# Interleaved RoPE on one core: row 2 stored and row 5 loaded in sixteen alternating pieces

## The chip, the cores and the metric

The kernel runs on one core of a Trainium2 chip. The metric is the device time of one execution in microseconds; before the change the median of three runs is 316.26 us (316.24 to 316.33). In the profile DVE is VectorE, ACT is ScalarE, POOL is GpSimd, SP is SyncE. POOL and SP issue the transfers of this kernel, each on a queue of its own (q0 is POOL's, q1 is SP's); sixteen DMA engines carry them out.

## The reference

The kernel rotates pairs of neighbouring elements (rotary position embedding, interleaved form). The input `x` has 8 batch rows of 2048 positions, 16 heads and 64 elements, in fp32; one batch row is 8 MB.

```python
x1 = x_pairs[..., 0]; x2 = x_pairs[..., 1]      # neighbours along the head dimension
out1 = x1 * cos - x2 * sin                      # cos, sin: [2048, 32], the same for all batches and heads
out2 = x1 * sin + x2 * cos
out = np.stack([out1, out2], axis=-1).reshape(batch, seq_len, num_heads, head_dim)
```

## The kernel before

A batch row is spread over 128 partitions, each of which holds K = 16 neighbouring positions: 16 x 1024 elements, a contiguous 64 KB in DRAM and 32 KB in SBUF, where the data lie in bf16. Transfers on POOL's queue convert between fp32 and bf16 on the way. SBUF has five slots for batch rows (`xt`); row b lives in slot `HOME[b]`, with `HOME = [0, 1, 2, 3, 4, 0, 1, 2]`. So rows 5, 6 and 7 take the slots of rows 0, 1 and 2 once those have been stored. In what follows rows count from 0: the third row is row 2, the sixth is row 5.

`load(b, n)` (L63) and `store(b, n)` (L67) each issue a single DMA on POOL for n whole rows. `rotate` does a row with three VectorE instructions: a product with the sine table into a work tile (L82), a product in place with the cosine table (L83), and their sum, with neighbours swapped (L88).

The order is written out by hand; each engine runs its instructions in the order of the program, and waits for what an instruction needs:

- SP loads the first four positions of row 0 in fp32 (L92). POOL issues the rest of row 0 (L93), cos and sin (L94, L95), rows 1 and 2 as one transfer, row 3, then row 4 in two parts (L98, L99).
- VectorE builds the tables (L103 to L105) and rotates row 0. A one-element copy on ScalarE (L111, L112) holds back `store(0, 1)` until the loads are nearly over; a one-element copy on POOL (L116, `mark`) waits for the last part of row 4.
- After it POOL issues `store(1, 2)`, `load(5, 1)`, `load(6, 2)`. `load(5, 1)` needs slot 0, so it waits for the store of row 0; `load(6, 2)` needs slots 1 and 2, so it waits for the store of rows 1 and 2.
- Rows 3 and 4 are rotated and stored as one transfer, rows 5 and 6 likewise, and row 7 in two parts: 12 positions from POOL (L127), and the last four through an fp32 tile and SP (L132, L133). L131 holds that last copy back until rows 5 and 6 are stored.

Of the kernel before, what the change touches and what calls it, by code (L numbers as in the profile page):

```python
# [2 lines left out]

# [4 lines left out]


@with_exitstack  # L10
def kernel(
    ctx: ExitStack,
    tc: tile.TileContext,
    x: bass.AP,
    cos: bass.AP,
    sin: bass.AP,
    out: bass.AP,
):
    nc = tc.nc
    fp32 = mybir.dt.float32  # L20
    bf16 = mybir.dt.bfloat16
    mult = mybir.AluOpType.mult
    add = mybir.AluOpType.add

    B, S, H, D = x.shape
    P = 128
    K = S // P
    KP = 16
    D2 = D // 2
    HD = H * D  # L30
    NX = 5
    HEAD = 4
    TAIL = 4
    LAST = 2


    HOME = [0, 1, 2, 3, 4, 0, 1, 2]

    x_t = x.rearrange("b (p k) h d -> b p k (h d)", p=P, k=K)
    out_t = out.rearrange("b (p k) h d -> b p k (h d)", p=P, k=K)  # L40
    x_r = x.rearrange("b (p k) h d -> p b (k h d)", p=P, k=K)
    out_r = out.rearrange("b (p k) h d -> p b (k h d)", p=P, k=K)
    cos_t = cos.rearrange("(p k) c -> p (k c)", p=P, k=K)
    sin_t = sin.rearrange("(p k) c -> p (k c)", p=P, k=K)

    consts = ctx.enter_context(tc.tile_pool(name="consts", bufs=1))
    stage = ctx.enter_context(tc.tile_pool(name="stage", bufs=1))

    xt = consts.tile([P, NX, K * HD], bf16)
    cos_sb = consts.tile([P, K * D2], fp32)  # L50
    sin_sb = consts.tile([P, K * D2], fp32)
    c_tab = consts.tile([P, K, D], bf16)
    s_tab = consts.tile([P, K, D], bf16)

    gate = consts.tile([1, 1], bf16)
    mark = consts.tile([1, 1], bf16)

    def home(b, k0=0, k1=K):
        return xt[:, HOME[b], k0 * HD : k1 * HD].rearrange("p (k c) -> p k c", c=HD)

    def load(b, n):
        h = HOME[b]
        nc.gpsimd.dma_start(out=xt[:, h : h + n], in_=x_r[:, b : b + n])  # L63

    def store(b, n):
        h = HOME[b]
        nc.gpsimd.dma_start(out=out_r[:, b : b + n], in_=xt[:, h : h + n])  # L67

    def rotate(b, k0=0, k1=K):
        nk = k1 - k0  # L70
        xp = home(b, k0, k1)
        qt = stage.tile([P, KP, HD], bf16, name="qt", tag="work")

        def rows(a):
            return a.rearrange("p k (h e) -> p k h e", h=H, e=D)

        def tab(a):
            return dataclasses.replace(
                a, offset=a.offset + k0 * D, ap=[a.ap[0], [D, nk], [0, H], [1, D]]
            )  # L80

        nc.vector.tensor_tensor(out=rows(qt[:, :nk]), in0=rows(xp), in1=tab(s_tab), op=mult)  # L82
        nc.vector.tensor_tensor(out=rows(xp), in0=rows(xp), in1=tab(c_tab), op=mult)  # L83
        q_swap = dataclasses.replace(
            qt, offset=qt.offset + 1, ap=[qt.ap[0], [2, nk * HD // 2], [-1, 2]]
        )
        x3 = xp.rearrange("p k (a j) -> p (k a) j", j=2)
        nc.vector.tensor_tensor(out=x3, in0=x3, in1=q_swap, op=add)  # L88

    with tc.manual_schedule():  # L90
        head = stage.tile([P, TAIL, HD], fp32, name="st", tag="work")
        nc.sync.dma_start(out=head[:, :HEAD], in_=x_t[0, :, :HEAD])  # L92
        nc.gpsimd.dma_start(out=home(0, HEAD), in_=x_t[0, :, HEAD:])  # L93
        nc.gpsimd.dma_start(out=cos_sb, in_=cos_t)  # L94
        nc.gpsimd.dma_start(out=sin_sb, in_=sin_t)  # L95
        load(1, 2)
        load(3, 1)
        nc.gpsimd.dma_start(out=home(4, 0, K - LAST), in_=x_t[4, :, : K - LAST])  # L98
        nc.gpsimd.dma_start(out=home(4, K - LAST), in_=x_t[4, :, K - LAST :])  # L99

        nc.scalar.copy(out=home(0, 0, HEAD), in_=head[:, :HEAD])  # L101
        s2 = s_tab.rearrange("p k (i j) -> p (k i) j", j=2)
        nc.vector.tensor_copy(out=s2[:, :, 0], in_=sin_sb)  # L103
        nc.vector.tensor_scalar_mul(s2[:, :, 1], sin_sb, -1.0)  # L104
        nc.vector.tensor_copy(  # L105
            out=c_tab.rearrange("p k (i j) -> p (k i) j", j=2),
            in_=cos_sb.to_broadcast([P, K * D2, 2]),
        )
        rotate(0, 0, HEAD)
        rotate(0, HEAD, K)  # L110
        nc.scalar.copy(out=gate, in_=home(4, K - LAST - 1, K - LAST)[:1, 0, :1])  # L111
        nc.scalar.copy(out=xt[:1, HOME[0], :1], in_=xt[:1, HOME[0], :1])  # L112
        store(0, 1)
        rotate(1)
        rotate(2)
        nc.gpsimd.tensor_copy(out=mark, in_=xt[:1, 4, K * HD - 1 :])  # L116
        store(1, 2)
        load(5, 1)
        load(6, 2)
        rotate(3)  # L120
        rotate(4)
        store(3, 2)
        for b in range(5, B):
            rotate(b)
            if b == 6:
                store(5, 2)
        nc.gpsimd.dma_start(out=out_t[B - 1, :, : K - TAIL], in_=home(B - 1, 0, K - TAIL))  # L127

        tail = stage.tile([P, TAIL, HD], fp32, name="st", tag="work")
        last = home(B - 1, K - TAIL, K)  # L130
        nc.scalar.copy(out=xt[:1, HOME[B - 2], :1], in_=xt[:1, HOME[B - 1], K * HD - 1 :])  # L131
        nc.scalar.copy(out=tail, in_=last)  # L132
        nc.sync.dma_start(out=out_t[B - 1, :, K - TAIL :], in_=tail)  # L133


# [1 line left out]
_INS = ['x', 'cos', 'sin']  # L137
_OUTS = [((8, 2048, 16, 64), 'float32')]


# [23 lines left out]
```

## Time and profile before

| | |
|---|---|
| median of three runs | 316.26 us (316.24 to 316.33) |
| span of the profiled execution, first to last instruction | 314.4 us |
| around it (median less span) | 1.8 us |
| VectorE busy | 210.4 us, 67% |
| ScalarE busy | 8.9 us, 3% |
| POOL busy | 13.9 us, 4%, 19 instructions |
| DMA | 102.24 MB written in 2816 packets, mean 325 GB/s |
| HBM | 67.63 MB read, 67.11 MB written, 429 GB/s |

The profile gives no time of its own for the profiled execution beside its span; the 1.8 us are what the median of the timed runs has on top. The GB/s of the DMA rows count the bytes that are written: 4 MB for a row that is loaded to bf16, 8 MB for one that is stored in fp32. On POOL and SP an instruction DMA_DIRECT2D is the issue of a transfer, not the transfer.

### The profile page before, as it was taken

What the parts mean: (1) busy time and instruction counts of PE and PEld (TensorE: products, weight loads), DVE (VectorE), ACT (ScalarE), POOL (GpSimd) and SP (SyncE); (2) the same over time, 40 slices, a digit from 0 to 9 for tenths busy, and PEclk for the clock granted to TensorE, in tenths of its full rate; (3) what the DMA queues carried; (4) which work ended last, traced back from release to release, by engine and by line L of the source; (5) the groups of instructions that cost most, each with busy time, mean ns of one, the idle gap of its engine ahead of it and who ended that gap; (6) DMA issues with size and microseconds to landing.
All of it is one profiled execution on the core that took longest, in us unless ns stands there. A gap on an engine that the chain in (4) does not pass through costs nothing.

```text
span 314.4 us, 116 instructions
## 1 busy us (share of the span) xinstructions
DVE 210.4 (67%) x30; ACT 8.9 (3%) x6; POOL 13.9 (4%) x19
## 2 busy tenths in 40 slices
DVE  0009995099999999999992399903999999200000
ACT  1040000000000000000000000000000000000400
POOL 5000000000002400000000000000000000000000
DMA  7999999999999999999999999999999999999997
GB/s 254 263 283 200 200 200 267 200 200 213 229 233 258 425 509 400 400 459 475 400 200 246 221 200 200 254 213 333 400 525 409 400 400 525 409 400 400 434 434 333
DMA packets 2816, 102.24 MB, mean 325 GB/s; under 512 B 256, under 2 KB 256, under 8 KB 512
## 3 DMA queue, kind: packets, MB, share of 16 engines
q0 software_dynamic: 2528, 98.04, 96.8%
q1 hardware_dynamic: 288, 4.19, 3.3%
HBM read 67.63 MB, written 67.11 MB: 429 GB/s over the span
## 4 chain that ended last, share of the span: by engine, by line
another core or an unknown queue 87%; DMA 5%; ACT 1%; ACTq 1%; issue 0%
DMA st<-in_x_dram 5%; ACT xt L101 1%; ACTq L159 1%; ACT xt L131 0%; ACT xt L112 0%; ACTq L131 0%; ACT gate L111 0%
## 5 line engine op out<-in xcount | busy, mean ns | idle before, releaser
L82 DVE TENSOR_TENSOR qt<-xt,s_tab 128x16384 bf16<-128x16384 bf16 (+2 forms) x9 | 69.7, 7743 | 34.4 <-DMA xt<-in_x_dram 34.3
L83 DVE TENSOR_TENSOR xt<-xt,c_tab 128x16384 bf16<-128x16384 bf16 (+2 forms) x9 | 69.7, 7744 | 0.4
L88 DVE TENSOR_TENSOR xt<-xt,qt 128x16384 bf16<-128x16384 bf16 (+2 forms) x9 | 69.7, 7744 | 0.3
L103 DVE CAST s_tab<-sin_sb 128x512 bf16<-128x512 f32 x1 | 0.5, 458 | 23.8 <-DMA sin_sb<-in_sin_dram 23.8
L67 POOL DMA_DIRECT2D out_dram<-xt x4 | 2.7, 671 | 185.5 <-ACT xt L112 93.8
L131 ACT COPY xt<-xt 1x1 bf16<-1x1 bf16 x1 | 0.2, 193 | 195.4 <-DMA out_dram<-xt 195.4
L116 POOL COPY mark<-xt 1x1 bf16<-1x1 bf16 x1 | 5.0, 5014 | 1.4 <-DMA xt<-in_x_dram 1.4
L63 POOL DMA_DIRECT2D xt<-in_x_dram x4 | 2.6, 656 | 43.0 <-DMA out_dram<-xt 43.0
L101 ACT CAST xt<-st 128x4096 bf16<-128x4096 f32 x1 | 3.6, 3604 | 13.3 <-DMA st<-in_x_dram 13.3
L132 ACT CAST st<-xt 128x4096 f32<-128x4096 bf16 x1 | 3.6, 3598 | 0.0
L111 ACT COPY gate<-xt 1x1 bf16<-1x1 bf16 x1 | 0.2, 193 | 79.7 <-DMA xt<-in_x_dram 79.7
L127 POOL DMA_DIRECT2D out_dram<-xt x1 | 0.6, 572 | 25.5 <-DVE xt L88 25.5
L101 ACT ACT_TABLE_LOAD x1 | 1.3, 1283 | 0.7 <-PEq L148 0.7
L93 POOL DMA_DIRECT2D xt<-in_x_dram x1 | 0.7, 680 | 0.8 <-PEq L159 0.8
L105 DVE CAST c_tab<-cos_sb 128x1024 bf16<-128x1024 f32 x1 | 0.7, 684 | 0.0
L99 POOL DMA_DIRECT2D xt<-in_x_dram x1 | 0.6, 592 | 0.0
L98 POOL DMA_DIRECT2D xt<-in_x_dram x1 | 0.6, 586 | 0.0
L95 POOL DMA_DIRECT2D sin_sb<-in_sin_dram x1 | 0.6, 562 | 0.0
L94 POOL DMA_DIRECT2D cos_sb<-in_cos_dram x1 | 0.6, 554 | 0.0
L104 DVE TENSOR_SCALAR s_tab<-sin_sb 128x512 bf16<-128x512 f32 x1 | 0.4, 445 | 0.0
L112 ACT COPY xt<-xt 1x1 bf16<-1x1 bf16 x1 | 0.2, 189 | 0.0
L148 POOL MEMSET const-float32-0.0<- 128x1 f32 x1 | 0.1, 93 | 0.2 <-issue 0.2
(3 smaller groups left out, 0.3 us busy)
## 6 DMA issues: line engine op xcount, KB each, us to landing
xt<-in_x_dram POOLq DMA_DIRECT2D x2, 8192.0 KB, 58.5
xt<-in_x_dram POOLq DMA_DIRECT2D x2, 4096.0 KB, 67.6
out_dram<-xt POOLq DMA_DIRECT2D x1, 6144.0 KB, 40.9
xt<-in_x_dram POOLq DMA_DIRECT2D x1, 3584.0 KB, 94.3
xt<-in_x_dram POOLq DMA_DIRECT2D x1, 3072.0 KB, 21.2
st<-in_x_dram SPq DMA_DIRECT2D x1, 2048.0 KB, 14.5
out_dram<-st SPq DMA_DIRECT2D x1, 2048.0 KB, 15.5
xt<-in_x_dram POOLq DMA_DIRECT2D x1, 512.0 KB, 96.3
```

Source lines behind the costliest of these rows:

```text
L63: nc.gpsimd.dma_start(out=xt[:, h : h + n], in_=x_r[:, b : b + n])
L67: nc.gpsimd.dma_start(out=out_r[:, b : b + n], in_=xt[:, h : h + n])
L82: nc.vector.tensor_tensor(out=rows(qt[:, :nk]), in0=rows(xp), in1=tab(s_tab), op=mult)
L83: nc.vector.tensor_tensor(out=rows(xp), in0=rows(xp), in1=tab(c_tab), op=mult)
L88: nc.vector.tensor_tensor(out=x3, in0=x3, in1=q_swap, op=add)
L93: nc.gpsimd.dma_start(out=home(0, HEAD), in_=x_t[0, :, HEAD:])
L94: nc.gpsimd.dma_start(out=cos_sb, in_=cos_t)
L101: nc.scalar.copy(out=home(0, 0, HEAD), in_=head[:, :HEAD])
L105: nc.vector.tensor_copy(out=c_tab.rearrange("p k (i j) -> p (k i) j", j=2), in_=cos_sb.to_broadcast([P, K * D2, 2]),)
L116: nc.gpsimd.tensor_copy(out=mark, in_=xt[:1, 4, K * HD - 1 :])
L132: nc.scalar.copy(out=tail, in_=last)
L159: with _tile.TileContext(nc) as tc:
```

## The change

`store(1, 2)` is taken apart: row 1 is stored alone, in one transfer. Row 2 is then stored one position at a time. For each of the 16 positions POOL issues a store of that position of row 2 (128 partitions x 1024 elements, 4 KB of fp32 in each partition, 512 KB in all) and behind it a load of the same position of row 5, which is as large. `load(6, 2)` becomes two transfers of a row each. Nothing else is changed, and VectorE, ScalarE and SP have the same instructions as before.

```diff
         nc.gpsimd.tensor_copy(out=mark, in_=xt[:1, 4, K * HD - 1 :])
-        store(1, 2)
-        load(5, 1)
-        load(6, 2)
+        store(1, 1)
+        for k in range(K):
+            nc.gpsimd.dma_start(out=out_t[2, :, k], in_=home(2, k, k + 1)[:, 0])
+            nc.gpsimd.dma_start(out=home(5, k, k + 1)[:, 0], in_=x_t[5, :, k])
+        load(6, 1)
+        load(7, 1)
         rotate(3)
         rotate(4)
         store(3, 2)
```

On POOL three transfers become 35. A transfer has a completion counter out of eight, which POOL's transfers take in rotation.

## The prediction

> **What bounds the kernel now.** I read the page's summary and its forty slices first, then the windows of two stretches with one kind of transfer only, then the timeline, then the DMA issues.
>
> ```profile
> span 314.4 us, 116 instructions
> DVE 210.4 (67%) x30; ACT 8.9 (3%) x6; POOL 13.9 (4%) x19
> ...
> DMA  7999999999999999999999999999999999999997
> ...
> q0 software_dynamic: 2528, 98.04, 96.8%
> q1 hardware_dynamic: 288, 4.19, 3.3%
> HBM read 67.63 MB, written 67.11 MB: 429 GB/s over the span
> ...
> another core or an unknown queue 87%; DMA 5%; ACT 1%; ACTq 1%; issue 0%
> ```
> The DMA row is 9 in every slice but the first and last: the sixteen DMA engines never rest, VectorE does a third of the time. The chain that ended last is 87% "unknown queue", which here is the GpSimd DMA queue q0. So the time is the sum of the DMA work; nothing else can move it unless it makes that queue run dry.
>
> ```profile
> 24.00:80.00 56.00, 45.11 (x12) 0.00 (x0) 0.00 (x0) 1.00 1.00 215
> 222.00:254.00 32.00, 31.86 (x5) 0.00 (x0) 0.70 (x1) 1.00 0.99 426
> ```
> Windows: the last two columns are DMA share and GB/s by bytes written. The first holds loads alone (fp32 to bf16: 215 written is 430 read), the second stores alone (426 written). Either way the fp32 side runs at some 428 GB/s.
>
> ```profile
> 121.00 0.56 POOL L63 DMA_DIRECT2D xt<-in_x_dram  x1 [5.19 <-DMA out_dram<-xt]
> ...
> 159.37 0.71 POOL L63 DMA_DIRECT2D xt<-in_x_dram  x1 [37.81 <-DMA out_dram<-xt]
> ...
> 178.41 8.69 DVE L82 TENSOR_TENSOR qt<-xt,s_tab 128x16384 bf16<-128x16384 bf16 x1 [11.16 <-DMA xt<-in_x_dram]
> ...
> 217.01 8.69 DVE L82 TENSOR_TENSOR qt<-xt,s_tab 128x16384 bf16<-128x16384 bf16 x1 [12.45 <-DMA xt<-in_x_dram]
> ...
> 294.33 0.19 ACT L131 COPY xt<-xt 1x1 bf16<-1x1 bf16 x1 [195.43 <-DMA out_dram<-xt]
> ```
> The timeline gives the price of a row: rows 6 and 7 load from 178.41 to 217.01, 19.3 us each; rows 3 to 6 are stored from 217.01 to 294.33, again 19.3 us each. Row 5's load is queued at 121.00 but runs from about 159 (behind the store of rows 1 and 2) to 178.4.
>
> ```profile
> cos_sb<-in_cos_dram POOLq DMA_DIRECT2D x1, 256.0 KB, 21.2
> sin_sb<-in_sin_dram POOLq DMA_DIRECT2D x1, 256.0 KB, 21.3
> ```
> Two small transfers that stood in a queue: issued at 1.93 and 2.47, they land at 23.1 and 23.8, some 0.64 us apart. 256 KB at 428 GB/s is 0.61.
>
> **The change, step by step.** The bytes are the same; only the 19.3 us store of row 2 and the 19.3 us load of row 5 are cut, into 16 pieces each, of 512 KB on the fp32 side (1.2 us). For prices finer than the page prints I use the trace's records of single DMA packets on one engine (a packet is here one partition's run; each engine has 8 partitions).
>
> 1. *More, shorter packets.* From one start to the next a 64 KB packet takes 2412 ns, load or store; the 56 KB ones of L98 2111; the 16 KB ones of the last fp32 store 607; the 8 KB ones of L99 305; the 4 KB ones of cos and sin 156. So 37.6 ns per KB and 4 to 6 ns per packet. A run becomes 16 packets of 4 KB. At 156 that is 2496, +84 ns; at 150.4+4 it is 2470, +58. Eight partitions, two rows: +0.9 to +1.3 us, all of it on the DMA engines and so on the path. I take 1.1, between the 8 KB casting packets and the 4 KB plain ones. Upper bound: a packet's own duration, not its spacing, which is 20 ns longer for the bf16 loads (2432) and 37 ns for the stores (2449); if short packets did not overlap at all, 128 x (20+37) ns = +7.3 us more. Lower bound: none of it is lost, 0.
>
> 2. *More transfers, each ending in a semaphore write on every engine.* In the packet records a store that is followed by a load costs 41 ns extra (158.64 to 158.68 on the last engine), a load followed by a store 21 less the 19 by which the first store packet is shorter (2393), thus 2, store after store 41-19 = 22, load after load 20. New are 15 store-to-load turns (0.62 us), 15 load-to-store (0.03), one store to store (row 1 to 2) and one load to load (6 to 7): 0.69 us, on the path.
>
> 3. *32 more issues on the GpSimd queue, in place of a part of two.* An issue there takes 0.55 to 0.74 us (L94 0.554, L67 0.671 mean). Of themselves they are hidden, 32 x 0.7 = 22 us of an engine that is busy for 14 of 314, as a piece takes 1.25 us to move. What counts is that the queue stays filled. The compiled order gives these DMAs eight completion counters in rotation, and each one that is used again waits for the transfer eight places before. So: row 1's store is issued at 115.1, row 2's first piece at 115.8, row 5's first at 121.0 (it needs row 0's slot), the next five by about 124.5. Then the queue holds row 1's store and seven pieces, and the eighth piece waits for row 1's store, till about 139.8. Behind that wait stand all later pieces, loads 6 and 7 and store(3,2). But seven pieces are 8.7 us of work, and the notice of a landing reaches POOL within 0.6 us (row 0's store lands by 120.44, L63 runs at 121.00); an issue is turned into packets within 1.2 us of its start (store(0) issued at 99.19, packets from 100.37, beside a running VectorE instruction). Refilling takes 2.5 us at most, against 8.7. Cost: 0; without that cover, see rival C.
>
> 4. *load(6,1), load(7,1), store(3,2).* load(6) waits for an earlier piece (about 170), load(7) for row 2's last (about 178.5), and store(3,2), ready before at 167.55, goes behind it at about 179. Each is queued while load(6) still runs (180 to 199), so: 0.
>
> 5. *VectorE.* Row 5 is complete at 178.4+1.8 = 180.2, where it was 178.4; row 6, which used to wait for 6 and 7 together, is now there at 199.5, so rotate(6) runs from 206.3, not 217.0, and rotate(7) from 232.5, not 243.2. That is worth nothing: store(5,2) was issued at 243.46 and its first packet ran at 255; it only waits longer in the queue. No loss either: ScalarE's L131 waits for that store.
>
> Sum: 1.1+0.7 = +1.8 us, span 314.4 to 316.2. Outside the span lie 316.26-314.43 = 1.83 us of the median, taken as unchanged: 316.26+1.8 = 318.1.
>
> The Trainium skill, "DMA: Bandwidth & Descriptors", section Rules for kernel authors, asks for 1 MiB or more per DMA, and its fit under Anatomy of one DMA gives 2.0 us plus bytes/436 GB/s: 512 KB would take 3.2 us, and 32 of them in turn (an estimate from that page) +64 us. The trace disagrees where transfers stand in a queue: cos and sin, half that size, land 0.64 us apart.
>
> **The rivals.**
>
> *B: reads and writes overlap; faster.* A load reads 64 KB and writes 32, a store reads 32 and writes 64. Taken in turn finely enough, each direction would carry 96 KB per pair where now 128 KB pass one after the other: 38.6 us becomes 29.0, 9.6 less, 306.7+1.8 = 308.5 if complete. Against it: the turns that the trace already has show nothing of it. The first packet after a turn takes 2411 (load) or 2393 ns (store) against 2412, and neighbours overlap by only 20 to 37. Each piece also ends in the same semaphore write as those turns. To decide, a turn would have to save over 58 ns (1.8 us/31). Chance 0.07. The same page of the Trainium skill, section Two DMAs through the same engine are not ordered, says that an engine's read and write sides are separate queues and that descriptors are pipelined; that speaks for B, and the 19 ns above is all that this trace shows of it.
>
> *C: the queue runs dry; much slower.* If an issue took longer from wait to packets than the transfer does, the 25 pieces behind the first wait would run at the pace of issuing. With 8.7 us in hand this starts at 1.25+8.7/25 = 1.6 us per issue; at 2 us it costs 25 x 0.75-8.7 = +10 us (328). For it: at the very start seven issues from 1.25 on gave their first packet at 5.44. Against it: the longest issue is 0.74, and store(0) had packets after 1.2. Chance 0.06.
>
> *D: 4 KB casting packets cost more than plain ones.* No row shows them; the bound in step 1 gives up to +9 us (325). The 8 KB casting loads with 305 ns speak against it. Chance 0.12 for over 320.
>
> *E: the pieces cost nothing.* Pairs share a packet, the turns hide each other: under 0.63 us, which is 0.2% and about what this measurement can tell from no change. Step 2 alone gives 0.69. Chance 0.06. That the change does not do what it says I can leave out: the order on the GpSimd queue is the written one, and one queue is served in order in every row of the trace.
>
> **How the numbers follow.** Forecast (1.2 to 3.5 us slower) 0.69, B 0.07, C 0.06, D 0.12, E 0.06. The likeliest time is 318.1. The forecast's own range is 317.5 to 319.8; to 8 in 10 I go down to 316.9 (part of E) and up to 320.8 (the nearer part of D). Slower 0.69+0.06+0.12 = 0.87, same 0.06, faster 0.07.
>
> **What would show it.** Right: DMA still 9 in all slices, span near 316.2, POOL busy about 35 us; L82's idle time down from 34.3 to about 23 (10.7 before row 1, 13 before row 5, none before 6 and 7), and rotate(5) about 1.8 us later than 178.4. POOL's wait for row 1's store ends near 140. C would show as a lower DMA digit between 140 and 180, D as full digits with rotate(5) after 182, B as rotate(5) before 178. The prediction is wrong if rotate(5) is on time and the span is not, or the reverse: the loss or gain is then not in the pieces.

## The result, and the profile after

The changed kernel takes 318.12 us (317.92 to 318.32, four runs) where the kernel before takes 316.29: a ratio of 1.0056 (95% interval 1.0044 to 1.0068), so 1.83 us slower. The forecast was 318.1, within 316.9 to 320.8. The profiled execution ran 317.98 us with a span of 316.2.

The page of the changed kernel, the lines that answer to those of before:

```profile
span 316.2 us, 158 instructions
DVE 210.3 (67%) x30; ACT 8.9 (3%) x6; POOL 30.4 (10%) x51
...
DMA  7999999999899999999999999999999999999997
...
q0 software_dynamic: 6880, 98.04, 98.9%
...
HBM read 67.63 MB, written 67.11 MB: 426 GB/s over the span
...
L82 DVE TENSOR_TENSOR qt<-xt,s_tab 128x16384 bf16<-128x16384 bf16 (+2 forms) x9 | 69.7, 7743 | 23.4 <-DMA xt<-in_x_dram 23.2
...
out_dram<-xt POOLq DMA_DIRECT2D x16, 512.0 KB, 9.7
...
xt<-in_x_dram POOLq DMA_DIRECT2D x16, 256.0 KB, 9.7
```

The same bytes go at 426 GB/s instead of 429, in 6880 packets on q0 instead of 2528. The DMA row is full in the slices of the pieces (17 to 22, counted from 0); its one 8, at 79 to 87 us, lies ahead of the change. VectorE has its 210 us, but waits 23.4 us instead of 34.4 before L82: no gain, as it is not what bounds the kernel. The last two lines show the depth of the queue: a piece lands 9.7 us after its issue, and eight pieces of 1.25 us are 10.

The timeline of the changed kernel, from POOL's wait for row 1's store to the end of the stores of rows 5 and 6:

```profile
123.65 0.55 POOL L119 DMA_DIRECT2D out_dram<-xt  x1
...
140.08 0.54 POOL L120 DMA_DIRECT2D xt<-in_x_dram  x1 [15.88 <-DMA out_dram<-xt]
...
141.31 0.53 POOL L119 DMA_DIRECT2D out_dram<-xt  x1 [0.69 <-DMA out_dram<-xt]
142.49 0.53 POOL L120 DMA_DIRECT2D xt<-in_x_dram  x1 [0.65 <-DMA xt<-in_x_dram]
...
171.28 0.53 POOL L63 DMA_DIRECT2D xt<-in_x_dram  x1 [0.79 <-DMA out_dram<-xt]
179.05 0.53 POOL L63 DMA_DIRECT2D xt<-in_x_dram  x1 [7.24 <-DMA out_dram<-xt]
179.57 0.71 POOL L67 DMA_DIRECT2D out_dram<-xt  x1
179.84 8.69 DVE L82 TENSOR_TENSOR qt<-xt,s_tab 128x16384 bf16<-128x16384 bf16 x1 [12.63 <-DMA xt<-in_x_dram]
...
206.02 8.69 DVE L82 TENSOR_TENSOR qt<-xt,s_tab 128x16384 bf16<-128x16384 bf16 x1
...
295.72 0.19 ACT L134 COPY xt<-xt 1x1 bf16<-1x1 bf16 x1 [196.83 <-DMA out_dram<-xt]
```

After seven pieces POOL waits till 140.08 for the eighth, and from then on idles 0.6 to 0.9 us before each issue: it waits for the transfers, not they for it. Rotate(5) starts at 179.84 instead of 178.41, and the stores of rows 5 and 6 are over at 295.72 instead of 294.33. So 1.4 us are lost between 121 and 180, and nothing is won or lost between there and 296. The rest of the 1.78 us by which the span grew comes at the very end. SP's waits there (line, what it waited for, us, times, longest), first in the kernel before, then in the changed one:

```profile
SPq L159 <- PEq L159: 0.6, 2, 0.4
```

```profile
SPq L162 <- DMA out_dram<-st: 2.8, 1, 2.8
SPq L162 <- PEq L162: 1.0, 2, 0.8
```

The wait for the last store is 2.8 us as before, but the exchange between the engines after it took 1.0 us where it took 0.6.

### The profile page after: what moved, and what is told of

Same layout as the page of the kernel before. It is cut to its first block, busy times and chain, and to the rows that moved or that the text cites. A ratio compares the mean times of both kernels' runs of the same rounds, so it can differ in the third digit from the quotient of the medians.

```text
span 316.2 us, 158 instructions
## 1 busy us (share of the span) xinstructions
DVE 210.3 (67%) x30; ACT 8.9 (3%) x6; POOL 30.4 (10%) x51
## 3 DMA queue, kind: packets, MB, share of 16 engines
q0 software_dynamic: 6880, 98.04, 98.9%
## 4 chain that ended last, share of the span: by engine, by line
another core or an unknown queue 62%; ACTq 1%; ACT 0%; issue 0%
ACTq L162 1%; ACT xt L134 0%; ACTq L134 0%
## 5 line engine op out<-in xcount | busy, mean ns | idle before, releaser
L82 DVE TENSOR_TENSOR qt<-xt,s_tab 128x16384 bf16<-128x16384 bf16 (+2 forms) x9 | 69.7, 7743 | 23.4 <-DMA xt<-in_x_dram 23.2
L67 POOL DMA_DIRECT2D out_dram<-xt x4 | 2.5, 629 | 146.0 <-ACT xt L112 93.8
L120 POOL DMA_DIRECT2D xt<-in_x_dram x16 | 8.6, 535 | 29.0 <-DMA out_dram<-xt 21.3
L119 POOL DMA_DIRECT2D out_dram<-xt x16 | 8.5, 534 | 17.9 <-DMA out_dram<-xt 9.4
L63 POOL DMA_DIRECT2D xt<-in_x_dram x4 | 2.4, 604 | 8.0 <-DMA out_dram<-xt 8.0
L130 POOL DMA_DIRECT2D out_dram<-xt x1 | 0.5, 547 | 25.5 <-DVE xt L88 25.5
L93 POOL DMA_DIRECT2D xt<-in_x_dram x1 | 0.7, 680 | 0.8 <-PEq L162 0.8
L99 POOL DMA_DIRECT2D xt<-in_x_dram x1 | 0.6, 594 | 0.0
L98 POOL DMA_DIRECT2D xt<-in_x_dram x1 | 0.6, 586 | 0.0
```

Of the source, the lines that this page charges most:

```text
L119: nc.gpsimd.dma_start(out=out_t[2, :, k], in_=home(2, k, k + 1)[:, 0])
L120: nc.gpsimd.dma_start(out=home(5, k, k + 1)[:, 0], in_=x_t[5, :, k])
```

## The experiments

Each code excerpt stands against the changed kernel, the one with the second queue against the kernel before; "..." stands for code left out.

**The price by the size of a piece.** The theory (T), read off the packet records of the changed kernel after the result, says that each pair of pieces costs some 86 ns of DMA time. Pieces of two positions, then of half a position:

```diff
-        for k in range(K):
-            ... out_t[2, :, k] ... x_t[5, :, k]
+        for k in range(0, K, 2):
+            nc.gpsimd.dma_start(out=out_t[2, :, k : k + 2], in_=home(2, k, k + 2))
+            nc.gpsimd.dma_start(out=home(5, k, k + 2), in_=x_t[5, :, k : k + 2])
```

> Pieces of two positions, 8 stores and 8 loads in turn instead of 16 and 16. T: the changed kernel's pair takes 2498 ns where a sixteenth of both rows takes 2412, so 86 ns per pair whatever its size: 8 x 86 + 42 ns = +0.73 us, 317.0 us, rotate(5) at 179.1. Rival (R3): the cost is not per piece but comes once (a wait at the start of the pieces, or something outside the queue): 318.0 as with sixteen. Rival (B): coarser turns lose some overlap: not below 318.

Measured: 316.95 us, ratio 1.0022 (1.0012 to 1.0031), +0.70 against 316.25; rotate(5) at 179.32 in a trace whose earlier marks (L112) stand 0.2 later than before. T holds; R3 (the cost comes once) and B (finer turns overlap more) fall.

```diff
+        W = HD // 2
         for k in range(K):
+            for c in range(0, HD, W):
                 ... [..., c : c + W] of the store and of the load
```

> Pieces of half a position (2 KB of fp32 in a partition, 256 KB), 32 stores and 32 loads in turn. T: 32 x 86 ns + 42 = +2.8 us, 319.1 us; +2.3 if two of the 2 KB runs share a packet as those of cos and sin do. The queue still does not run dry: a piece takes 0.66 us to move, an issue on POOL 0.53. Rival (C), that the issuing with its wait takes more than 0.66 us: from +5 us, 321 and above, with gaps in the DMA row between 145 and 185. Rival (B), finer turns overlap more: below 318.

Measured: 319.37 us, 1.0097 (1.0084 to 1.0111), +3.12, no slice of the pieces under 9. This is 0.3 over T: a single 8 KB packet of q14, the queue of kind "instruction", stood on one engine at 168.4 for 0.34 us, and that engine ran 0.30 us late from then on. The packet records give the finer number, from one end-of-transfer semaphore write to the next (median of the engines):

| piece | store | load | pair | the same bytes in whole rows | excess per pair |
|---|---|---|---|---|---|
| 1 MB (two positions) | 2429 ns | 2478 ns | 4907 | 4823 | 84 ns |
| 512 KB (the change) | 1225 | 1273 | 2498 | 2412 | 86 |
| 256 KB (half a position) | 622 | 671 | 1293 | 1206 | 87 |

The excess hardly depends on the size: it is the price of a transfer in a full queue, not of a byte.

**The cost doubled.** The first try put row 1's store in pieces too, with row 5's load between, then row 2 with row 6:

```diff
-        store(1, 1)
-        for k in range(K):
-            ... store of row 2, load of row 5
-        load(6, 1)
+        for r in (1, 2):
+            for k in range(K):
+                ... store of row r, load of row r + 4
```

> The suspected cost doubled: row 1 is stored in turn with row 5's load, and row 2 in turn with row 6's load, 64 pieces of one position; row 7 whole. T: 32 pairs x 86 ns = +2.75 us, 319.0 us, rotate(5) at 158.4 + 1.4 = 159.8 or as soon as VectorE is free (167.3). Rival (R3), that the cost comes once: 318.0. Rival (B): lower than 318.

Measured: 325.84 us, 1.0305 (1.0287 to 1.0323), +9.6: against every expectation. The order, not the pieces, is to blame. Row 5's first piece must wait for row 0's store with only one piece queued behind that store, and row 7's load for row 2's last piece with only one piece left. The packet records show the queue empty from 121.5 to 122.4, and from 203.4 (the slowest engine both times) to 204.3. The first piece of row 5 takes 3.80 us there in place of 1.27, and row 7 takes 23.2 in place of 19.3: 6.4 of the 6.8 us over T. The next kernel has as many pieces, but always a whole row in the queue where a wait comes:

```diff
-        load(7, 1)
         rotate(3)
+        for k in range(K):
+            ... store of row 3, load of row 7
         rotate(4)
-        store(3, 2)
+        store(4, 1)
```

> The cost doubled once more, now without emptying the queue: pieces of row 2's store and row 5's load in turn as in the changed kernel, load(6) whole, then pieces of row 3's store and row 7's load in turn, row 4 stored whole. T: 32 pairs x 86 ns and some 0.05 us for the split rows, +2.8 us, 319.1 us, DMA digits 9 throughout. Rival (R3), the cost comes once: 318.0. If the 6.8 us that the first kernel with two rows of pieces lay above T (325.84) come from the pieces and not from its emptied queue: over 322.

Measured: 319.39 us, 1.0096 (1.0082 to 1.0110), +3.06 against 316.33, and the pairs of both rows take 2498 ns again. Twice the pieces cost twice the 1.4 us; the 0.3 beyond that is again one instruction packet, of 0.32 us on one engine at 208.7.

**The split of the rows alone.**

```diff
-        for k in range(K):
-            ...
+        store(2, 1)
+        load(5, 1)
```

> No pieces: rows 1 and 2 are stored and rows 5, 6 and 7 loaded in one transfer each, five instead of three. T: one more store after store (22 ns) and one more load after load (20 ns): +0.04 us, 316.3 us, rotate(5) at 178.4, rotate(6) without a wait at 204.6. Rival (R3), that the splitting of the two-row transfers, and with it the waits and counters that move, makes part of the change's loss: 316.6 to 317.

Measured: 316.34 us, 1.0003 (0.9994 to 1.0012), +0.09. The loss is in the pieces (R3 falls).

**The turns.** The same 32 pieces, stores first:

```diff
         for k in range(K):
             ... store of row 2
+        for k in range(K):
             ... load of row 5
```

> The same 32 pieces, but the 16 stores of row 2 come first and the 16 loads of row 5 behind them, so that one turn from store to load is left of sixteen. Theory (T): what costs is the fixed price of a piece on each DMA engine, its last semaphore write and its shorter packets, and the turn itself is nothing: store after store 22 ns and load after load 20 ns against 43 ns for a pair of turns, so as slow as the changed kernel, 318.0 us (317.8 to 318.3), rotate(5) at 179.8. Rival (R1): the change of direction is what costs; then the 0.7 us of the turns go, 317.3. Rival (B), that alternating overlaps reads and writes a little: slower than the changed kernel, over 318.5.

Measured: 319.29 us, 1.0097 (1.0083 to 1.0111), 1.2 us more than in turn. The time alone is the one that B gave (over 318.5), and T and R1 missed it. The packet records divide it, and they do not bear B out. Store pieces in a row take 1245 ns, load pieces 1253, together again 2498: the price of a pair is the same without turns, as T has it, so turns neither cost nor save, and R1 and B fall. But the 13th and 14th store take 1605 and 1716 ns. The timeline shows it on POOL, whose waits between two issues grow from 0.7:

```profile
153.99 0.53 POOL L121 DMA_DIRECT2D xt<-in_x_dram  x1 [0.73 <-DMA out_dram<-xt]
155.66 0.53 POOL L121 DMA_DIRECT2D xt<-in_x_dram  x1 [1.15 <-DMA out_dram<-xt]
157.52 0.53 POOL L121 DMA_DIRECT2D xt<-in_x_dram  x1 [1.33 <-DMA out_dram<-xt]
```

Three more kernels followed that up: the same one once more, and each half alone.

> The kernel with the 16 stores first and the 16 loads behind them once more, for its trace: if the stalled store packets stand again near 155 us, they belong to the order of the transfers, and the time is 319.3 again. If they are gone or elsewhere and the time is near 318.0, they were a disturbance of that chip.

Measured: 319.19 us, 1.0090 (1.0076 to 1.0105); the same two pieces take 1566 and 1672 ns. POOL's waits in its timeline:

```profile
155.59 0.53 POOL L121 DMA_DIRECT2D xt<-in_x_dram  x1 [1.24 <-DMA out_dram<-xt]
157.50 0.53 POOL L121 DMA_DIRECT2D xt<-in_x_dram  x1 [1.38 <-DMA out_dram<-xt]
```

So it belongs to that order and is no accident of one run.

```diff
         for k in range(K):
             ... store of row 2
+        load(5, 1)
```

> Row 2 is stored in 16 pieces one after the other, row 5 is loaded whole behind them. From the changed kernel's packets (T): a piece of the store takes 1204 ns and 41 for its semaphore write, 16 of them 19.92 us where the whole row takes 19.30: +0.62, with the split rows +0.66, 316.9 us. Rival (R4), formed after the kernel with stores first and loads then measured 319.3, 1.3 over T: a run of short stores of its own stalls the engines, as in the two stretches at 154.9 and 156.4 of that trace; then 318 or more, with store packets of over 300 ns.

Measured: 317.40 us, 1.0035 (1.0022 to 1.0047), +1.07. Twelve stores take 1245 ns, the last four 1277 to 1285 (mean of the engines).

```diff
+        store(2, 1)
         for k in range(K):
             ... load of row 5
```

> Row 2 is stored whole, row 5 is loaded in 16 pieces one after the other. T: a piece of the load takes 8 x 154 + 21 ns, 16 of them 20.05 us for 19.30: +0.75, with the split rows +0.79, 317.1 us. Rival (R4): the same 317.1, since it has no run of short stores. If the additional 1.3 us of stores first and loads then belong to the loads: 318 or more.

Measured: 317.23 us, 1.0032 (1.0021 to 1.0044), +0.90. Every load at 1253 ns but the first, after the store, at 1273. Here T is nearly met. In the store half the stall begins at the same piece, but is smaller: 0.15 us as the mean of the engines, against 0.76 and 0.70 with the load pieces behind. The last engine to finish, for which the next wait waits, loses 0.43 against 0.98 and 0.89, and 0.43 is about what this kernel lies above T's 316.9. So R4 is half right at best: a run of short stores stalls by itself, and about twice as long with the load pieces queued behind it. What stalls the engines there is not settled; no instruction packet stands there, and no kernel with the pieces in turn shows it.

**Do reads and writes overlap?** In one queue every piece ends in a semaphore write. The last chance of rival B is two queues. ScalarE copies half of row 3 to an fp32 tile and SP stores it:

```diff
         rotate(3)
+        for k in range(0, 8, 2):
+            nc.scalar.copy(out=side, in_=home(3, k, k + 2))
+            nc.sync.dma_start(out=out_t[3, :, k : k + 2], in_=side)
         rotate(4)
-        store(3, 2)
+        nc.gpsimd.dma_start(out=out_t[3, :, 8:], in_=home(3, 8, K))
+        store(4, 1)
```

> The kernel before, but positions 0 to 7 of row 3 are copied on ScalarE to an 8 KB fp32 tile, two at a time, and stored from SP's queue (four transfers of 1 MB) beside the loads of rows 5, 6 and 7 on POOL's queue; cos and sin share that tile. Each engine then has stores and loads of two queues to take in turn, packet by packet, with no semaphore write between. T (an engine carries one packet after another, whichever way it goes): no gain, +0.1 to +0.5 us for the additional packets, 316.4 to 316.8. Rival (B), that an engine can read for one queue while it writes for the other: each MB of store under the loads is hidden, up to 3 x 2.4 = 7 us, 309 to 315.

Measured: 316.77 us, 1.0017 (1.0007 to 1.0026), +0.50. From its timeline:

```profile
142.92 84.17 SPq L124 DMA_DIRECT2D out_dram<-side  x4
...
171.22 1.90 ACT L123 CAST side<-xt 128x2048 f32<-128x2048 bf16 x1 [28.33 <-DMA out_dram<-side]
181.62 8.69 DVE L83 TENSOR_TENSOR qt<-xt,s_tab 128x16384 bf16<-128x16384 bf16 x1 [14.38 <-DMA xt<-in_x_dram]
...
197.90 1.90 ACT L123 CAST side<-xt 128x2048 f32<-128x2048 bf16 x1 [24.78 <-DMA out_dram<-side]
...
224.66 8.69 DVE L83 TENSOR_TENSOR qt<-xt,s_tab 128x16384 bf16<-128x16384 bf16 x1 [16.89 <-DMA xt<-in_x_dram]
224.83 1.90 ACT L123 CAST side<-xt 128x2048 f32<-128x2048 bf16 x1 [25.03 <-DMA out_dram<-side]
```

The packets of the second and third MB of stores run beside loads, from 177.8 to 197.5 and 204.4 to 224.2 (the first MB runs half beside stores and half beside loads, the fourth beside stores). In the packet records an engine takes one store packet of 8 KB (0.32 us), then one load packet, and 2.73 us after the first the next store packet: the 0.32 and the 2.41 of a load, one after the other. Had they been hidden, the time would have fallen by up to 4.8 us. The loads pay for them: rows 6 and 7 arrive at 224.66, 43.0 us after row 5, where they took 38.6. B falls.

**How near is the empty queue?** Quarter positions, 128 pieces:

```diff
+        W = HD // 4
         for k in range(K):
+            for c in range(0, HD, W):
                 ... [..., c : c + W] of the store and of the load
```

> Pieces of a quarter of a position (1 KB of fp32 in a partition, 128 KB), 64 stores and 64 loads in turn. T alone, with the queue always filled: 64 x 86 ns + 42 = +5.5 us, 321.8 us. T with the limit of rival C from its other side: a piece takes 0.34 us to move but 0.53 to issue, so from about 140 on the 121 pieces left come at POOL's pace, 121 x 0.53 = 64 us, where they would need 42; rotate(5) at about 204 and 342 us, with the DMA digits down to 6 or 7 from 140 to 204. If issuing with its wait takes 0.65, 356.

Measured: 347.86 us, ratio 1.0999 (1.0977 to 1.1021). The page's row of POOL, and the timeline:

```profile
POOL 4000000000033030899999881000000000000000
...
142.12 0.57 POOL L122 DMA_DIRECT2D xt<-in_x_dram  x1
142.64 0.57 POOL L121 DMA_DIRECT2D out_dram<-xt  x1
143.16 0.58 POOL L122 DMA_DIRECT2D xt<-in_x_dram  x1
```

No wait stands before an issue any more; they come every 0.52 us, and the transfers at that pace. C is right here, with its expected price a little low: rotate(5) starts at 208.80, 4.8 us after the 204 expected. The DMA digit does not show it (9 in most slices): the packet records, which overlap, add up to a share of 1.18 from 142 to 204, the same as in the changed kernel's pieces from 142 to 176. The rate does show it, with 182 GB/s written against 315.

The price of a queue that is really empty:

```diff
-            nc.gpsimd.dma_start(out=home(5, k, k + 1)[:, 0], in_=x_t[5, :, k])
+            nc.gpsimd.dma_start(out=home(7, k, k + 1)[:, 0], in_=x_t[7, :, k])
         ...
-        load(6, 1)
-        load(7, 1)
+        load(5, 1)
+        load(6, 1)
```

> The pieces of row 7, not row 5, are loaded between those of row 2's store, into the very slot that is being emptied; rows 5 and 6 are loaded whole after it. Each piece's load now waits for the store just before it, so the queue is empty at every pair until POOL has had the notice (up to 0.6 us) and the issue has become packets (up to 1.2 us). T: 16 x 1.3 to 1.8 us = +21 to +29 us on top of +1.4, 338 to 347 us, DMA digits between 5 and 7 for some 65 us. This is the price of a transfer that does not stand in a queue. Rival (C2), that the changed kernel already pays part of this: a small difference, below 328.

Measured: 374.75 us, 1.185 (1.183 to 1.187), +58.5: twice what was expected. DMA digits, and the timeline:

```profile
DMA  8999999999999985756667575989998999999997
...
141.41 0.54 POOL L120 DMA_DIRECT2D xt<-in_x_dram  x1 [25.65 <-DMA out_dram<-xt]
141.93 0.53 POOL L119 DMA_DIRECT2D out_dram<-xt  x1
...
147.28 0.54 POOL L120 DMA_DIRECT2D xt<-in_x_dram  x1 [4.81 <-DMA out_dram<-xt]
```

A pair comes every 5.9 us, 3.4 more than in the full queue. By the packet records the store ends at 140.8, POOL issues at 141.4, the first packets start at 142.65, and the engines are at their pace only from about 144.2, since the first two rounds of packets take up to 1.5 us each. The expectation had the first two terms (1.3 to 1.8 us) and lacked the third.

## Why the prediction was right

*Step 1, the packets: mis-sized.* +1.1 us was taken, between 0.9 and 1.3; it is 0.69. In the changed kernel a 4 KB store packet comes every 152.9 ns and a load packet every 154.0, so 8 x (152.9+154.0) - 2412 = 43 ns per pair, 16 times. That is 2.2 and 3.3 ns a packet over the 150.75 that 4 KB take in a whole row, where 4 to 6 had been taken. The row it leaned on, the 4 KB packets of cos and sin at 156 ns, is not one of 4 KB runs: each of these transfers has 64 packets for 128 partitions, so a packet holds two runs of 2 KB. Rival D falls with this (casting packets of 4 KB take no longer than the plain ones of cos and sin), and E as well, as the loss is there.

*Step 2, the semaphore writes: right.* Expected 41+2 ns per pair of turns, found 43: a store piece of 1204 ns, then 41, a load piece of 1231, then 22. The 1204 are 19 short of 8 x 152.9, as the prediction has it, and what a pair takes beyond its packets is 2498 - 8 x 306.9 = 43. In all 0.69 us. That they are no price of turning was not said there; it took the stores-first kernel to show it.

*Step 3, the queue: right.* POOL's wait ended at 140.08 (expected near 140). Issuing costs nothing at 1.25 us per piece, and much at 0.34. POOL was busy for 30.4 us, not 35: an issue takes 0.53 here, not 0.7.

*Steps 4 and 5: right.* load(6) at 171.28 (170), load(7) at 179.05 (178.5), store(3,2) at 179.57 (179); rotate(5) at 179.84 (180.2), rotate(6) at 206.02 (206.3), L82's idle time 23.4 (23).

*The sum: right in part by luck.* Steps 1 and 2 make 1.4 us in the traces, not 1.8. The other 0.4 stands after the last transfer, where no step looked (SP's wait for the engines, 1.0 against 0.6 us); without it the sum would have come out 0.4 high. It is in the spans of all four runs of the changed kernel (316.1 to 316.5, where 1.4 on top of 314.4 makes 315.8). With two positions it is not there, and in the profile of half positions that wait is 0.7, so it does not grow with the pieces. The traces show what it goes with. GpSimd pauses 0.36 us longer than before ahead of the 69th instruction that its records hold, one of those that end the program, and an 8 KB packet of the instruction queue follows. Both kernels with the stores first have the same pause ahead of the same 69th instruction, and the same packet at the end. The six kernels with at most 57 such instructions have neither. The other five have more than 80, and their packet comes between the 69th and the 74th, while the pieces run. From the last landing to the end of the span it is 0.86 to 0.96 us in these eleven, and 1.24 to 1.38 in the three. So the 0.4 us go with the 32 more issues after all, not through the queue, where step 3 put their cost at 0, but through the length of GpSimd's program. No run was made to test this alone.

The Trainium skill's "DMA: Bandwidth & Descriptors", section Rules for kernel authors, wants at least 1 MiB per DMA. In a full queue the runs here put a price of 86 ns on a pair of 512 KB pieces, 3.6% of their 2412. In the empty queue the fit on that page of the Trainium skill (section Anatomy of one DMA: 2.0 us plus bytes/436 GB/s) is nearer: 3.2 us for 512 KB as an estimate, where the loads behind their own store land 4.3 us after their issue:

```profile
xt<-in_x_dram POOLq DMA_DIRECT2D x16, 256.0 KB, 4.3
```

## What to carry to other kernels

Where the DMA queue is full in every slice, count what a change adds to the queue: here 40 to 50 ns for each more transfer, whatever its size from 256 KB to 1 MB, and nothing back for earlier data or for stores and loads in turn. What must be watched is whether a wait can empty the queue: look what is issued ahead of each wait, and compare the time between two issues (0.53 us) with that of moving one piece. Do not take the end of the program as unchanged either when an engine gets many more instructions. Of all these kernels none is faster than the one with the fewest transfers.

## What the runs showed of the hardware

- An engine moves 64 KB on the fp32 side in 2412 ns whether it loads or stores, and does not load for one queue while it stores for another (packets of the two queues stand one after the other; +0.5 us for 4 MB on a second queue, some 2.5 MB of them beside loads, no gain).
- A load that finds the queue empty costs 3.4 us here, more than the notice and the issue: the first packets are slow, up to 1.5 us for 2 KB written.
- A full DMA digit does not prove a fed queue: with quarter positions it stays at 9 mostly while the rate falls to 182 GB/s.
- An 8 KB instruction packet came once GpSimd had about 70 instructions on record: amid full queues it cost one engine 0.3 us, at the program's end the kernel 0.4.
- Sixteen 512 KB stores in a row with loads of pieces behind them stall at the 13th and 14th, by 0.83 and 0.75 us (medians of the engines) in two runs; in turn they never did. This stays open.
